# Hybrid decoder step on one core: the factors of four group norms sent as rows through DRAM instead of broadcast products, with new queue orders

## The chip, the core and the metric

The kernel runs on one core of one Trainium2 chip. A core has TensorE (PE, matmul and transpose, with its weight loads shown apart as PEld), VectorE (DVE), ScalarE (ACT), GpSimd (POOL) and SyncE (SP, which here only issues DMAs), each with an instruction queue of its own that runs in order. The metric is the device time in microseconds (us) of one execution. The time of the kernel before is 1998.02 us, the median of 3 runs (1997.06 to 2000.51).

## The reference

One layer of a decoder, for a prompt of 2048 tokens and 8 sample tokens with caches, model width 1024, all in fp32:

```
xn = rmsnorm(x, norm1_g)
xr, gr, q, k, v = split(xn @ w_in)              # 512, 512, 512, 128, 128 columns
rec = rglru(conv4(xr), ...) * gelu(gr)          # per-token scan, block-diagonal gates
att = sliding_window_attention(q, k, v, sinks)  # 8 heads, 2 kv heads, window 128
mix = concat(rmsnorm(rec, rec_norm_g), rmsnorm(att, attn_norm_g))
h   = x + mix @ w_out
hn  = rmsnorm(h, norm2_g)
y   = h + (silu(hn @ w_gate) * (hn @ w_up)) @ w_down
out = rmsnorm(y, final_norm_g)
```

The two norms inside `mix`, called group norms here, are what the change touches: each divides a token's 512 features by the root of their mean square (plus 1e-6) and multiplies by a gain per feature.

## The kernel before, in words

**Layout.** Features lie on the 128 partitions, tokens on the free axis. A tile of 128 features by some 512 tokens is called a chunk; `rec`, `att` and the like have four chunks c = 0 to 3. An fp32 product is done as three fp32r products of high and low parts (high·high, high·low, low·high), so every operand is split into a high part (a copy to fp32r on ScalarE) and a low part (the difference, mostly on VectorE).

**Stages.** The 2056 tokens are four sub-sequences s = 0 to 3: the first holds 512 prompt tokens and the 8 sample tokens (520, run as two blocks of 260), the others 512. Each goes through the input projection (14 units of 128 columns: 0 to 3 the recurrent branch, 4 to 7 the gelu gate, 8 keys, 9 values, 10 to 13 queries), the recurrence, the attention, the two group norms and the output projection (8 units). Work of neighbouring sub-sequences is interleaved, so that TensorE has, for instance, units of s = 1 while the norms of s = 0 are under way. This takes about the first 600 us. Then comes the FFN over three groups of tokens ("halves"), 11 pairs of 128-wide slices each, with sums of operands that save products, and the final norm.

**A group norm** (`group_norm`, line 1515 on). For one s and one group, named `rc` (recurrent) or `at` (attention):

1. ScalarE squares the four chunks, GpSimd adds them up.
2. `rstd_cols`: TensorE multiplies each stretch of w tokens by a column of averages (records named `st_...`), which leaves one factor per token, tokens on partitions, as w × nt numbers (w = 104, nt = 5 for s = 0, else 128 and 4). VectorE adds 1e-6 (line 1125) and GpSimd raises to the power −0.5 (line 1126). The result is `rccols` or `atcols`.
3. The factor of each token must now stand in all 128 partitions, tokens along the free axis. Line 1532 chooses between two ways. `row_bcast` does it on TensorE: nt products of one column, read as a w × 128 matrix, with the identity (records `bc_rc`, `bc_at`), into one PSUM bank of a pool that has only that bank (`ps_m`), and a ScalarE copy to SBUF (line 1140). A bank holds 512 numbers, so s = 0 needs four products, a copy, a fifth product and a second copy; the fifth product waits until the first copy has freed the bank. `dram_bcast` does it by DMA: one TensorE transpose (`tr_rc`, `tr_at`), a ScalarE copy of the nt × w row (line 1149), a DMA of the row to DRAM (line 1150), and a DMA that reads it back into 128 partitions (line 1156). Both DMAs are issued from SyncE.
4. For each chunk: VectorE multiplies by gain and factor (line 1542), ScalarE copies the high part (line 1544), VectorE subtracts for the low part (line 1545). High and low part are the operand `mix` chunk that the output projection reads, recurrent chunks as k = 0 to 3, attention chunks as k = 4 to 7.

Before, only the recurrent norms of s = 1 and s = 2 went through DRAM; the other six group norms used products. The norm of the input (`x`) of s = 1 to 3 and part of the final norm (`f`) use rows as well. For s = 3 the attention factor is applied late, behind the output projection.

```
def rows_out(row, cols, w, nt, name):
    ps = m_tile(f"tr_{name}")
    tr(f"tr_{name}", ps[:nt, :w], cols, ident[:w, :w])
    v = rowp.tile([8, P], F32, tag="row", name=f"row_{name}")[:nt, :w]
    nc.scalar.copy(v, ps[:nt, :w])
    nc.sync.dma_start(row.rearrange("o (j p) -> (o j) p", p=w), v)
...
    nc.sync.dma_start(out[:, :w * nt], row.to_broadcast([P, w * nt]))
```

**The order of the work.** The instruction streams are made by generators with planned times, but the final order on each of the five queues is written out by hand in the table `ORDER` (TensorE from line 107, VectorE 547, ScalarE 668, GpSimd 750, SyncE 787), and `order_engines` ties each instruction to the one before it. A key names a stream: `rn0` and `an0` are the recurrent and the attention norm of s = 0 (DMAs too), `ip1_7_0` an input unit of s = 1, `op0_0_0` an output unit of s = 0, `r13` and `g13` a recurrent and a gate chunk, `a111` an attention step, `o01` an output unit's loads and sums, `x2` the input norm of s = 2. So when a sequence of keys is changed, an engine that stands at one instruction keeps all that follow it waiting.

**Around the change, in s = 0.** The profiled execution has the products of the recurrent factor at 195.34 to 196.4 us on TensorE, its first use on VectorE at 198.38, the eps addition of the attention factor at 211.05, its products from 214.55, the fifth product at 219.93, the first use at 220.71, and the first pass of the output projection at 222.65. Weight loads of the next input units (`w_in<-split_w`, line 1054) and raw loads of `w_out` stand on SyncE's queue in the same stretch.

Of the kernel before, what the change touches and what calls it, by code (L numbers as in the profile page):

```python
# [2383 lines left out]
```

## Time and profile before

| | us |
|---|---|
| median of 3 runs | 1998.02 |
| profiled execution, whole | 1999.11 |
| its span | 1997.0 |
| TensorE busy | 1971.0 |
| VectorE busy | 1560.6 |
| ScalarE busy | 981.3 |
| GpSimd busy | 959.8 |

The profile is of one execution. Its span runs from the first to the last recorded instruction; the whole time has 2.1 us more around it. A row of a group of instructions gives line, engine, operation, output <- inputs by the program's names, partitions × elements, count, then the busy time in us and the mean of one in ns, then the idle time of the engine just before such instructions and what ended it. A row of a timeline gives start and length in us, and in brackets the idle time before it with its releaser. A row of waits gives engine, instruction, what it waited for, the total in us, the number of times, and the longest. Matmuls are pipelined, so the lengths of their records overlap. In rows of DMA issues (SPq) the length is that of the issue and not of the transfer. The mean granted TensorE clock of the run is 0.997 of full speed.

### The profile page before, as it was taken

What the parts mean: (1) busy time and instruction counts of PE and PEld (TensorE: products, weight loads), DVE (VectorE), ACT (ScalarE), POOL (GpSimd) and SP (SyncE); (2) the same over time, 40 slices, a digit from 0 to 9 for tenths busy, and PEclk for the clock granted to TensorE, in tenths of its full rate; (3) what the DMA queues carried; (4) which work ended last, traced back from release to release, by engine and by line L of the source; (5) the groups of instructions that cost most, each with busy time, mean ns of one, the idle gap of its engine ahead of it and who ended that gap; (6) DMA issues with size and microseconds to landing.
All of it is one profiled execution on the core that took longest, in us unless ns stands there. A gap on an engine that the chain in (4) does not pass through costs nothing. (4 is left out here: it accounts for less than half of the span.)

```text
span 1997.0 us, 34846 instructions
## 1 busy us (share of the span) xinstructions
PE 1971.0 (99%) x12112; PEld 1874.8 (94%) x12112; DVE 1560.6 (78%) x2894; ACT 981.3 (49%) x2032; POOL 959.8 (48%) x821
## 2 busy tenths in 40 slices
PE   8999999999999999999999999999999999999998
PEld 8988898888877999999999999999999999999998
DVE  7887986777986888888998786886668586766776
ACT  6775774664664534444446433433345433433433
POOL 5412362130233896788998754534456423322323
PEclk9999999999999999999999999999999999999999
DMA  8873586576688978655667886776558675565552
GB/s 314 287 252 138 194 300 198 183 254 210 223 283 291 335 263 268 220 215 210 246 241 279 265 289 231 234 237 210 191 191 267 228 259 199 179 211 195 180 181 103
DMA packets 218470, 461.93 MB, mean 231 GB/s; under 512 B 26230, under 2 KB 90406, under 8 KB 218278
## 3 DMA queue, kind: packets, MB, share of 16 engines
q1 hardware_dynamic: 214662, 456.69, 67.4%
q10 hardware_dynamic: 3632, 3.02, 0.4%
q8 instruction: 95, 1.56, 0.3%
q14 instruction: 81, 0.66, 0.1%
HBM read 345.51 MB, written 115.17 MB: 231 GB/s over the span
## 5 line engine op out<-in xcount | busy, mean ns | idle before, releaser
L1070 PE MATMUL ps_g<-hn,w_g 128*128 128x342 f32 (+1 forms) x2772 | 569.4, 320 | 0.3 <-DMA w_g<-split_g 0.3
L1070 PE MATMUL ps_u<-hn,w_u 128*128 128x342 f32 (+1 forms) x2772 | 559.5, 320 | 1.5 <-DMA w_u<-split_u 0.9
L1070 PEld LDWEIGHTS ps_g<-hn,w_g 128*128 128x128 f32 x2772 | 461.3, 188 | 1.2 <-ACT wd L1972 0.5
L1070 PEld LDWEIGHTS ps_u<-hn,w_u 128*128 128x128 f32 x2772 | 459.5, 188 | 3.0 <-ACT c_u L2115 1.6
L2175 DVE TENSOR_TENSOR y<-y,pw 128x342 f32<-128x342 f32 (+1 forms) x756 | 359.1, 504 | 114.7 <-PE pw L1070 108.4
L1070 PE MATMUL ip<-xn,w_in 128*128 128x512 f32 (+1 forms) x1680 | 365.2, 357 | 6.1 <-ACT xn L1105 5.7
L1070 PEld LDWEIGHTS ip<-xn,w_in 128*128 128x128 f32 x1680 | 269.6, 189 | 45.8 <-ACT xn L1105 5.7
L1070 PE MATMUL pw<-fh,wd 128*128 128x342 f32 (+1 forms) x864 | 253.4, 320 | 0.5 <-DVE y L2175 0.5
L1070 PE MATMUL pw<-t,wd 128*128 128x342 f32 (+1 forms) x972 | 243.7, 320 | 2.8 <-DVE y L2175 2.7
L1070 PE MATMUL op<-mix,w_out 128*128 128x512 f32 (+1 forms) x960 | 205.8, 355 | 0.4 <-ACT mix L1544 0.4
L1070 PEld LDWEIGHTS op<-mix,w_out 128*128 128x128 f32 x960 | 157.5, 189 | 25.3 <-ACT mix L1544 0.8
L1070 PEld LDWEIGHTS pw<-t,wd 128*128 128x128 f32 x972 | 169.9, 188 | 4.9 <-DVE y L2175 4.0
L1973 POOL TENSOR_TENSOR wd<-rd,wd 128x512 fp32r<-128x512 f32 x85 | 121.8, 1434 | 103.4 <-ACT wd L1972 99.1
L1972 ACT CAST wd<-rd 128x512 fp32r<-128x512 f32 x159 | 98.6, 621 | 130.0 <-PE ps_u L1070 39.8
L1070 PEld LDWEIGHTS pw<-fh,wd 128*128 128x128 f32 x864 | 158.6, 188 | 1.2 <-DVE y L2175 0.8
L1904 POOL TENSOR_TENSOR w_u<-ru,w_u 128x512 fp32r<-128x512 f32 x44 | 61.4, 1395 | 170.2 <-ACT w_u L1903 95.9
L1070 PE MATMUL pw<-fl,wd 128*128 128x342 f32 (+1 forms) x432 | 132.9, 320 | 0.0
L2089 DVE TENSOR_TENSOR c_u<-c_u,ps_u 128x342 f32<-128x342 f32 (+1 forms) x99 | 50.2, 508 | 101.2 <-PE ps_u L1070 93.9
L2071 POOL TENSOR_TENSOR c_u<-c_u,c_g 128x342 f32<-128x342 f32 (+1 forms) x60 | 65.4, 1090 | 124.8 <-DVE c_u L2089 115.1
L2060 DVE TENSOR_TENSOR fl<-c_u,fh 128x342 fp32r<-128x342 f32 (+1 forms) x132 | 105.4, 803 | 17.7 <-ACT fh L2059 17.0
L2059 ACT CAST fh<-c_u 128x342 fp32r<-128x342 f32 (+1 forms) x132 | 63.0, 480 | 110.6 <-POOL c_u L2071 49.3
L1070 PE MATMUL pd<-fh,w_d 128*128 128x344 f32 (+1 forms) x384 | 92.9, 320 | 0.0
(319 smaller groups left out, 3490.7 us busy)
## 6 DMA issues: line engine op xcount, KB each, us to landing
w_g<-split_g SPq DMA_DIRECT2D x88, 512.0 KB
w_u<-split_u SPq DMA_DIRECT2D x88, 512.0 KB
w_in<-split_w SPq DMA_DIRECT2D x84, 512.0 KB
rg<-in_wgate SPq DMA_DIRECT2D x110, 256.0 KB
ru<-in_wup SPq DMA_DIRECT2D x110, 256.0 KB
w_out<-split_w SPq DMA_DIRECT2D x48, 512.0 KB
split_g<-w_g SPq DMA_DIRECT2D x44, 512.0 KB
split_u<-w_u SPq DMA_DIRECT2D x44, 512.0 KB
```

The lines of the kernel that those rows point to most:

```text
L1070: r = nc.tensor.matmul(*args, **kw)
L1904: lo_eng.tensor_tensor(w[:, 1, :], src, w[:, 0, :].bitcast(F32), op=ALU.subtract)
L1972: nc.scalar.copy(w[:, :, 0], v)
L1973: eng((E_DLO0, E_DLO1, E_DLO2)[gi][j]).tensor_tensor(w[:, :, 1], v, w[:, :, 0].bitcast(F32), op=ALU.subtract)
L2059: nc.scalar.copy(hi, v)
L2060: nc.vector.tensor_tensor(lo, v, hi.bitcast(F32), ALU.subtract)
L2071: (nc.vector if p == NPAIR - 1 or src is not v else eng(E_MUL[2 * h + n])).tensor_tensor(v, src, g, op=ALU.mult)
L2089: nc.vector.tensor_tensor(o, a, b, op)
L2175: nc.vector.tensor_tensor(v, v, ps, ALU.add)
```

## The change

Line 1532 chooses the way through DRAM for all group norms but the recurrent one of s = 3 and the late one (the attention norm of s = 3). So the attention norms of s = 0, 1 and 2 and the recurrent norm of s = 0 change from products to rows; the recurrent norms of s = 1 and 2 went through DRAM already.

```diff
-                bc = (dram_bcast if name == "rc" and s in (1, 2) else row_bcast)(cols[:w, :nt], w, nt, f"{name}{s}")
+                bc = (row_bcast if late or name == "rc" and s == 3 else dram_bcast)(cols[:w, :nt], w, nt, f"{name}{s}")
```

The table `ORDER` is written anew for all five engines. TensorE's list loses the 18 products `bc_at0`, `bc_at1`, `bc_at2`, `bc_rc0` and gains the four transposes; ScalarE's loses two entries (the second copies of s = 0); SyncE's gains eight (a write and a read for each of the four norms). All else is the same set of instructions in another order: of some 11,960 entries of TensorE 1357 stand elsewhere relative to the others, of VectorE's 2766 it is 745, of ScalarE's 1885 it is 402, of GpSimd's 817 it is 109, of SyncE's 1495 it is 304. The moves lie at the start (x loads, splits and the first input units), around the border of s = 0 and s = 1, and at some places in the FFN.

Around s = 0's norms, VectorE's list (`rn0` the four products and four low parts of the recurrent norm, `an0` first the eps addition and then products and low parts):

```diff
-a100+1 a100:3 a031 r11 a101+2 a101+2 v1 k2+1 a101:2 a111 k2+1 a101:2 a100 v1 a101:3 a110 a100 v1 a110:3 a120 rn0 a101
-a110:4 r12 a110 a111:4 rn0+6 rn0 a121 rn0+1 rn0 rn0+1 a111 a101 a111+1 rn0 g10 rn0+1 r10 g10 g11 r11 a111+1 rn0 g10
-r10 r11 g11 an0 r11 g11 r13 a111 g12 a111 g12 an0 an0+1 an0+2 an0 g13 g12 an0 an0+1 g13 an0:2 x2+1 x2 a100 o00:2 r11
+a100 a100+1 a100:3 a031 r11 a101+2 a101+2 v1 k2+1 a101:2 a111 k2+1 a101:2 a100 v1 a101:3 a110 a100 v1 a110:3 a120 rn0
+a101 a110 a110+1 a110+1 a110:2 a111:2 r12 a101 a111 a121 a111:2 a111+2 a111+2 a111+1 a111 r10 rn0 rn0+1 rn0 rn0+1 g10
+rn0 rn0+1 rn0 g10 g11 rn0 g10 r10 r11 g11 an0 r11:2 g12 g11 r13 g12 g13 g12 an0 an0+5 an0+1 an0 an0+1 an0:3 x2:2 a100
```

TensorE's list at the same places:

```diff
-s5_1_0:3 ip1_2_0 s5_1_1 ip1_2_0 pt4_1_1 s5_1_1 pt4_1_1:2 ip1_2_0 bc_rc0_0 s5_1_1 bc_rc0_0:3 pt4_1_1 ip1_5_0:2 o4_0_1
-ip1_5_0 bc_rc0_4 o4_0_1 s6_0_0 ip1_5_0:2 g1_0_0_0:2 ip1_6_0 g1_0_0_0 ip1_6_0:2 ip1_5_0 ip1_6_0:7 g1_0_1_0 ip1_6_0
...
-ip1_6_0 st_at0 ip1_3_0:4 st_at0 ip1_3_0:20 ip1_7_0:2 s6_0_1 ip1_7_0:3 pt5_0_0 ip1_7_0 bc_at0_0:4 ip1_7_0:7 pt5_0_0
-ip1_7_0 bc_at0_4 ip1_7_0:8 op0_0_0:2 ip1_7_0:2 g1_1_0_0 op0_0_0 g1_1_0_0 op0_0_0 g1_1_0_0 op0_0_0:8 op0_0_260:9
...
+s5_1_0 s5_1_1 s5_1_0:2 s5_1_1 ip1_2_0:2 pt4_1_1 s5_1_1 pt4_1_1:2 s5_1_0 s5_1_1 pt4_1_1 tr_rc0 ip1_2_0 ip1_5_0:2 o4_0_1
...
+ip1_6_0 st_at0 pt5_0_0 st_at0 pt5_0_0 s6_0_1 pt5_0_0 ip1_3_0:24 ip1_7_0:12 tr_at0 ip1_7_0:10 op0_0_0:2 ip1_7_0:2
```

SyncE's list there: the recurrent norm's write and read (`rn0:2`) stand ahead of the weight loads `r13:2 g13:2`, the attention norm's (`an0:2`) behind them.

```diff
-r12:2 g12:2 o01+3 r13:2 g13:2 o01+1 o00 o02 o00 o02+1 o01 o03 o01 o02 o03+1 x2:2 o04 o00 o04+1 o03 x2 o02+1 o01 o02 x2
+r12:2 g12:2 o01+3 rn0:2 r13:2 g13:2 an0:2 o01+1 o00 o02 o00 o02+1 o01 o03 o01 o03+1 o02 x2:2 o04 o00 o04+1 o03 o02 o01
```

More of the change, by code (lines that the diff above doesn't have):

```diff
@@ new lines @@
+vt0_0 ip0_3_0:6 ip0_3_1 ip0_3_0:2 ip0_3_1:4 ip0_11_0 vt0_1 ip0_3_1:13 ip0_11_0:6 ip0_3_1 vt0_2 ip0_3_1:4 ip0_11_0:7
+ip0_11_1 vt0_3 ip0_11_1:7 g0_0_0_0:2 ip0_11_1:4 g0_0_0_0 ip0_11_1:2 ip0_10_0:2 ip0_11_0 ip0_11_1:2 ip0_11_0
+g0_0_0_260:3 ip0_11_0:5 ip0_11_1 ip0_11_0 g0_0_1_0:3 ip0_11_0:2 ip0_10_0:4 ip0_11_1:4 g0_0_1_260:3 ip0_11_1:3
+ip0_10_0:3 ip0_10_1 ip0_10_0:5 ip0_10_1:7 ip0_10_0:9 ip0_10_1 ip0_10_0 ip0_10_1:13 ip0_13_0:2 ip0_10_1:2 ip0_13_0:12
+ip0_13_1:4 ip0_13_0:3 ip0_13_1:4 ip0_13_0:7 ip0_13_1:11 ip0_2_0 ip0_13_1:3 ip0_2_0 ip0_13_1:2 ip0_2_1:3 ip0_2_0:3
@@ new lines @@
+pt14_1_1:2 op2_7_0 pt14_1_1 op2_7_0:2 s15_1_1 op2_7_0:5 o14_1_0 op2_7_0:3 o14_1_0 op2_7_0:2 o14_1_1 st_rc3:4 op2_7_0
+o14_1_1 pt15_0_0:4 op2_7_0:4 bc_rc3_0:4 op2_7_0:2 pt15_0_1:4 op2_7_0 o15_0_0:2 o15_0_1 pt15_1_0:4 o15_0_1 st_h2:4
+pt15_1_1:4 o15_1_0:2 op3_0_0 op3_1_0 op3_2_0 op3_0_0:2 op3_1_0 o15_1_1 op3_2_0 op3_1_0:2 tr_h2 o15_1_1 op3_0_0
+op3_2_0:2 op3_1_0 op3_0_0 op3_1_0 op3_0_0:2 op3_2_0:2 op3_0_0:2 op3_1_0:2 op3_2_0:2 op3_1_0 op3_2_0:2 op3_0_0:3
+op3_1_0 op3_2_0 op3_1_0:2 op3_2_0 op3_3_0:12 op3_4_0:12 st_at3:2 op3_5_0:12 st_at3:2 op3_6_0:9 op3_7_0 op3_6_0:2
@@ new lines @@
+d0_1_6_0 d0_1_6_1 u0_2_1 d0_1_6_0:3 d0_1_7_0 d0_1_6_0 d0_1_7_0 d0_1_7_1 d0_1_7_0 d0_1_6_0 d0_1_7_0 d0_1_7_1:2
+d0_1_7_0:2 d0_1_7_1 u0_2_1 d0_1_7_1 u0_2_1 u0_2_2 u0_2_1 u0_2_2 d0_1_7_1 u0_2_2:3 u0_2_1 u0_2_2:7 u0_2_5:7 u0_2_6:2
+u0_2_5:3 u0_2_6 u0_2_5 u0_2_6:8 g0_3_1 u0_2_6 g0_3_1:3 u0_2_5 g0_3_1:7 u0_2_7 g0_3_1 u0_2_7:7 u0_2_3 u0_2_7 u0_2_3
+u0_2_7:3 u0_2_3:8 g0_3_6:2 u0_2_3 g0_3_6 u0_2_3 g0_3_6:9 u0_2_4:12 g0_3_2:10 d0_2_0_0 g0_3_2 d0_2_1_0 d0_2_0_0
+d0_2_0_1 d0_2_0_0 g0_3_2 d0_2_1_0:2 d0_2_0_1:2 g0_3_5 d0_2_1_1 g0_3_5 d0_2_1_1:2 g0_3_5:8 d0_2_0_1 d0_2_0_0 g0_3_5
@@ new lines @@
+w1_1_2_1 w1_1_1_2 w1_1_2_1 w1_1_1_3 g1_2_4 w1_1_1_2:2 g1_2_4:2 w1_1_1_3 g1_2_4 w1_1_4_1 g1_2_4 w1_1_4_1 w1_1_4_0
+g1_2_4 w1_1_4_1 w1_1_4_0 g1_2_4:3 w1_1_4_0 u1_2_1:2 g1_2_4 u1_2_1 g1_2_4:2 u1_2_1:3 w1_1_6_3 w1_1_6_2:2 u1_2_1:2
+u1_2_2:2 w1_1_6_3 w1_1_5_2 w1_1_6_2 w1_1_6_3 w1_1_5_2 w1_1_5_3 w1_1_5_2 w1_1_5_3:2 u1_2_1:2 u1_2_2 u1_2_1 u1_2_2
+u1_2_1 u1_2_2:6 w1_1_7_2 u1_2_2 w1_1_7_2 w1_1_7_3 w1_1_7_2 w1_1_3_2:2 w1_1_7_3 w1_1_3_2 w1_1_3_3 w1_1_7_3 w1_1_3_3
+w1_1_2_2:3 u1_2_6 u1_2_2 u1_2_6:2 w1_1_3_3 u1_2_6:7 w1_1_4_2 u1_2_6 w1_1_4_3 w1_1_4_2 u1_2_6 u1_2_5:2 w1_1_4_3
@@ new lines @@
+w2_9_2_2 u2_10_4:2 w2_9_4_2 w2_9_4_3 w2_9_4_2:2 w2_9_4_3:2 d2_10_0_1:2 u2_10_4 d2_10_1_1 d2_10_0_1:3 d2_10_1_1:5
+d2_10_2_1 d2_10_0_1 d2_10_2_1 d2_10_3_1 d2_10_2_1:2 d2_10_4_1 d2_10_2_1:2 d2_10_3_1:4 d2_10_4_1 d2_10_3_1 d2_10_5_1
+d2_10_4_1:4 d2_10_5_1 d2_10_6_1 d2_10_5_1:4 d2_10_6_1:5 d2_10_7_1:6 d2_10_0_0:5 d2_10_1_0:4 st_f2_1:6 d2_10_0_0
+d2_10_1_0:2 d2_10_2_0:3 bc_f2_1:3 d2_10_2_0:3 d2_10_3_0:6 d2_10_4_0:4 d2_10_5_0 d2_10_4_0:2 d2_10_5_0:3 d2_10_6_0
+d2_10_5_0:2 d2_10_6_0:5 d2_10_7_0:6 w_st_f2_0:9 w_bc_f2_0:3 st_f2_0:6 bc_f2_0:3
@@ L745 @@
[L745 to L748 removed]
+pre x0:2 pro+1 x0+1 x0+1 x0+2 x0+5 x0:2 x0+1 x0+2 x0+3 x0+5 x0+4 v0 x0+5 r01+1 x0 xs1 pre x0:4 v0 x0 k0 pro xs1 k0
```

1356 lines of the change are left out of this document (665 added, 691 removed).

## The prediction

> **What bounds the kernel now.** I read first the page, then the waits of TensorE, then a table by windows, and last the timelines around the places that the change touches.
>
> ```profile
> PE 1971.0 (99%) x12112; PEld 1874.8 (94%) x12112; DVE 1560.6 (78%) x2894; ACT 981.3 (49%) x2032; POOL 959.8 (48%) x821
> ```
> ```profile
> PE ip L1070 <- ACT xn L1105: 5.7, 1, 5.7
> PE pw L1070 <- DVE y L2175: 3.3, 5, 1.2
> PE bc_at L1070 <- ACT rb_at L1140: 2.4, 1, 2.4
> ```
> TensorE is busy nearly all of the 1997.0 us span. Its longest stall is the start; the longest inside the run is one stand of 2.4 us, before a product named bc_at, which the change takes out. So the time falls by what TensorE no longer issues, by that stand, and by what follows it; and it rises by whatever TensorE will then wait for.
>
> ```profile
> 217.60:219.90 2.30, 0.00 (x0) 0.00 (x0) 1.80 (x5) 1.02 (x2) 0.00 (x0) 1.00 0.79 312
> 221.50:224.80 3.30, 3.30 (x11) 2.72 (x10) 2.55 (x5) 2.71 (x5) 1.55 (x3) 0.50 0.00 0
> 200.00:300.00 100.00, 97.65 (x652) 88.70 (x651) 87.73 (x158) 74.80 (x147) 47.75 (x43) 0.98 0.72 248
> ```
> After the length come the busy times of TensorE, its weight loads, VectorE, ScalarE and GpSimd, then the granted clock, the share of the DMA engines and GB/s. TensorE stands for 2.3 us, and soon after it runs 3.3 us at half clock. In the stage 200 to 300 us VectorE is busy 87.7%: it has little room of its own, which matters below.
>
> **What is taken out of TensorE.** 18 products go: five each for the attention and the recurrent norm of sub-sequence 0, four each for the attention norms of 1 and 2. Four transposes come. Each fp32 product is two records.
>
> ```profile
> L1070 PE MATMUL bc_at<-cs,atcols 128*128 128x128 f32 (+1 forms) x34 | 5.3, 276 | 2.4 <-ACT rb_at L1140 2.4
> L1070 PE MATMUL bc_rc<-cs,rccols 104*128 104x104 f32 (+1 forms) x18 | 2.6, 271 | 0.0
> ```
> ```profile
> 439.77 1.80 PE L1070 MATMUL op<-mix,w_out 128*128 128x512 f32 x7
> 441.40 0.27 PE L1075 MATMUL tr_rc<-cs,rccols 128*4 128x128 f32 x1
> ...
> 594.18 0.94 PE L1070 MATMUL op<-mix,w_out 128*128 128x512 f32 x3
> 594.96 1.05 PE L1070 MATMUL bc_rc<-cs,rccols 128*128 128x128 f32 x8
> 595.77 0.94 PE L1070 MATMUL op<-mix,w_out 128*128 128x512 f32 x3
> ```
> Removed are 26 of the 34 bc_at records and 10 of the 18 bc_rc records. By busy time that is 26/34 of 5.3 and 10/18 of 2.6: 5.5 us. But records overlap, so I go by starts. Seven op passes take 441.40 − 439.77 = 1.63 us, 0.233 each. From 594.18 to 595.77 are 1.59 us, three op passes (0.70) and eight records of bc_rc: 0.111 each. 36 × 0.111 = 4.0 us. Four transposes at the same 0.11 are 0.45 us (at most 4 × 0.27 = 1.1 by the row at 441.40). All of it lies on TensorE, which has no other idle time to absorb it.
>
> **What goes with the stand.**
>
> ```profile
> 211.05 0.15 DVE L1125 TENSOR_SCALAR atcols<-st_at 104x5 f32<-104x5 f32 x1
> 211.83 5.47 DVE L1520 SCALAR_TENSOR_TENSOR rrec<-gt,rrec 128x512 f32<-128x512 f32 x1
> ...
> 220.71 2.10 DVE L1542 SCALAR_TENSOR_TENSOR ratt<-ratt,vec,rb_at 128x520 f32<-128x520 f32 x3 [0.50 <-ACT rb_at L1140]
> 228.30 2.41 DVE L1545 TENSOR_TENSOR mix<-ratt,mix 128x520 fp32r<-128x520 f32 x2
> ```
> ```profile
> 211.28 1.61 POOL L1126 TENSOR_TENSOR atcols<-atcols,nhalf 104x5 f32<-104x5 f32 x1 [14.42 <-DVE atcols L1125]
> 212.86 2.51 POOL L1044 TENSOR_TENSOR w_out<-raw_out,w_out 128x512 fp32r<-128x512 f32 x2
> ```
> ```profile
> 218.85 0.63 ACT L1517 ACTIVATE gt<-rrec 128x512 f32<-128x512 f32 x1 [6.34 <-DVE rrec L1434]
> 219.39 0.49 ACT L1140 COPY rb_at<-bc_at 128x416 f32<-128x416 f32 x1
> ```
> ```profile
> 219.93 0.47 PE L1070 MATMUL bc_at<-cs,atcols 104*128 104x104 f32 x2 [2.35 <-ACT rb_at L1140]
> ...
> 222.65 0.64 PE L1070 MATMUL op<-mix,w_out 128*128 128x260 f32 x2
> ```
> The fifth product needs the one bank of that pool, which the copy of the first four frees at 219.4 to 219.9. The copy stands on ScalarE behind a gelu step, and that one behind a VectorE operation that took 5.47 us while GpSimd ran without a break. With the rows there is one bank turn and no second copy, so the stand of 2.4 us goes. If no stand of this length takes its place, the 3.3 us at half clock go too: half of them is lost time, 1.7 us.
>
> The Trainium skill has a rule on that: "TensorE: Matmul & The Clock Gate", the section on the clock gate, says that the rate halves only after at least one whole idle window of about 3.4 us. By that rule a stand of 2.3 us should have cost no clock, and the sum below would be 1.7 us smaller. The trace differs from it, and I go by the trace.
>
> Without new waits the sum is 4.0 − 0.45 + 2.4 + 1.7 = 7.6 us: 6.1 in sub-sequence 0 (20 records 2.2, two transposes −0.2, stand 2.4, clock 1.7) and 1.6 in sub-sequences 1 and 2.
>
> **What the rows add.** Per norm: a transpose, a small ScalarE copy, and two DMAs on SyncE's queue, the read waiting until the write has landed. Two such trips of before had a consumer waiting for their end:
>
> ```profile
> 122.89 0.29 SPq L1150 DMA_DIRECT2D rows_x<-row_x  x1
> ...
> 125.82 0.32 SPq L1156 DMA_DIRECT2D rb_x<-rows_x  x1
> ...
> 1578.42 0.26 SPq L1150 DMA_DIRECT2D rows_f<-row_f  x1
> ...
> 1579.87 0.32 SPq L1156 DMA_DIRECT2D rb_f<-rows_f  x1
> ```
> ```profile
> 131.88 0.69 DVE L1434 TENSOR_TENSOR kraw<-ip,rb_x 128x512 f32<-128x512 f32 x1 [0.33 <-DMA rb_x<-rows_x]
> 1583.15 1.06 DVE L2195 SCALAR_TENSOR_TENSOR y<-y,vec,rb_f 128x342 f32<-128x342 f32 x2 [0.77 <-DMA rb_f<-rows_f]
> ```
> From the issue of the write to the consumer: 131.88 − 122.89 = 9.0 us and 1583.15 − 1578.42 = 4.7 us. The windows above show the DMA engines at 0.79 up to 219.9 us and at 0.00 from 221.5 to 224.8, so a broadcast at 220 finds them soon free: I take 6 us, nearer to the lower row, and keep both ends.
>
> The Trainium skill's page "DMA: Bandwidth & Descriptors", in its anatomy of a transfer, gives each about 2.0 us plus bytes over 436 GB/s and so speaks against splitting work into small transfers. An estimate from it, for a row and a 266 KB broadcast, is 2.0 + 2.6 = 4.6 us, the lower end of the two rows; by it first products would stand about 1.4 us earlier than I assume.
>
> Sub-sequence 0's recurrent norm: the transpose can stand where the products stood, at 195.34 in before; with the small copy the row write is issued at about 196.0, and its rows are in at 200.7 to 205.0.
>
> ```profile
> 195.34 0.37 PE L1070 MATMUL bc_rc<-cs,rccols 104*128 104x104 f32 x2
> ```
> ```profile
> 198.38 1.43 DVE L1542 SCALAR_TENSOR_TENSOR rrec<-rrec,vec,rb_rc 128x520 f32<-128x520 f32 x2
> ```
> ```profile
> 190.20 13.13 SPq L1054 DMA_DIRECT2D w_in<-split_w  x4
> ```
> The new VectorE order puts 7 to 14 other operations ahead of these four products; seven of about 0.68 us (the row at 131.88 is one of their kind) place the first at about 203.1 instead of 198.38. These products' results are read from 222.65 on, so the delay costs TensorE nothing itself. What it pushes is queued behind it on VectorE: the eps addition of the attention norm, which I place at 212.7 instead of 211.05, an estimate: of the operations moved ahead some wait for TensorE, which comes no sooner, so VectorE stands for some 1.7 us that it doesn't stand now. On SyncE the two DMAs stand ahead of the weight loads of the row at 190.20, which slip to about 198.6; the first user of those weights is at about 206, so a margin of 2 to 3 us covers it.
>
> Sub-sequence 0's attention norm: 212.7 + 0.15, then GpSimd's 1.6 (row at 211.28), transpose and copy: the write is issued at about 215.8. Rows in at 220.5 (4.7) to 224.8 (9.0), 221.8 at my 6 us. So the first attention product comes at about the time it had, 220.71, or 1 us later, while TensorE comes 6.1 us earlier. The last low part of before ended at 228.30 + 2.41 = 230.71, 10.0 us behind the first product. After, fewer gate operations stand between, and I allow 7.5 to 8.5 us: 229.3 to 230.3.
>
> ```profile
> 231.16 3.24 PE L1070 MATMUL op<-mix,w_out 128*128 128x260 f32 x25
> ```
> By the written order that last low part is read about the fifteenth pass of this block, at 232.9. So before had a slack of 2.2 us there, and 6.1 us are taken from it: TensorE arrives at 226.8 and waits until 229.3 to 230.3, which is 2.5 to 3.5 us in all, spread over the four chunks in pieces below 2.4, so without the clock. With 0.3 for other small waits behind the crowded VectorE, about 3.3 us of the 7.6 come back. Forecast: a gain of 4.3 us.
>
> Sub-sequences 1 and 2 gain 0.8 us each; VectorE delivers their attention halves several us before they are read, so the trip hides there. The rest of the change is order alone: at the start it moves x loads and splits, in the FFN it shifts neighbours by a few places. I cost both at nothing; the five waits of the row "DVE y L2175", 3.3 us in all, can go or come again, so ±2 us stay for the range.
>
> **The rivals.** (A) Full gain: the trips take about 4.7 us and VectorE, no longer starved as in the 5.47 us row, catches up; nothing stands. −7.6: 1990.4. For it: the starvation goes if GpSimd's run falls elsewhere. Against: the slack of 2.2 us.
>
> (B) The gain is used up in sub-sequence 0: the second trip takes 7 to 9 us, rows at 222.8 to 224.8, the last low part at about 232. TensorE waits some 5.5 us, in one piece long enough for half clock again, 1.7 more. −7.6 + 7.2 = −0.4: 1997.6. For it: the trip of 9.0 us. Against: that of 4.7.
>
> (C) Slower: VectorE stands in order at the first recurrent product. It decides from a first trip over 203.1 − 196.0 = 7.1 us. At 9.0 us VectorE stands 1.9 us, everything queued behind it slips, the attention row is written at 217.7, and after another 9.0 us the first product is at 226.7, the last low part 10 us later at 236.7 against 226.8: 9.9 us of waits and 1.7 of clock, and up to 1.9 of late gate steps. 13.5 − 7.6 = +5.9 at most, +4 without the gate steps; I take 2002.5.
>
> (D) The half clock at 221.5 does not come from the stand but falls where it falls, and stays: everything else as forecast, 1.7 less gain, 1995.4. For it: it begins 1.6 us after the stand has ended. Against: it occurs nowhere else in the run outside its two ends. The Trainium skill's clock page, in the same section, calls the window free-running, and under its rule the stand of 2.3 us cannot have been the whole cause.
>
> (E) The order alone moves the start or the FFN by more than the two norms do: either sign, 1990 to 2003, by the 3.3 us of small waits and the 5.7 us of the start's.
>
> **How the numbers follow.** Chances: forecast 0.42, A 0.19, B 0.22, C 0.08, D 0.05, E 0.04. The profiled execution took 1999.11 us, its span 1997.0 and 2.1 around it; the sum gives it 1994.8. The median of the runs is 1998.02, so its forecast is 1998.02 − 4.3 = 1993.7. About 0.2%, 4.0 us, is what a measurement of this kernel can tell from no change: faster means below 1994.0, slower above 2002.0. The forecast's own range, from the trip's two ends and the ±2 us, is 1991 to 1996.5; a little over half of it counts as faster, all of A, none of B, C or D, a quarter of E. Faster 0.42 × 0.57 + 0.19 + 0.01 = 0.44, slower C and a quarter of E, 0.09, the same 0.47. The range reaches to A's full gain and B: 1990.0 to 1998.0, which leaves C and parts of A and E out.
>
> **What would show it.** Right: no record of bc_at before the late sub-sequence; no wait on L1140 near 220; TensorE waiting in pieces of 0.3 to 2 us for mix or ratt of L1542 to L1545 between 222 and 232, near full clock there; rb_at of sub-sequence 0 landing 5 to 7 us after its row was issued. Wrong: no such waits (A); one piece above 2.3 us followed by half clock (B); VectorE idle before L1542 near 203 for rb_rc (C); half clock near 221 without a stand (D); a difference that arises before 190 us or after 600 us (E).

## The result and the profile after

Over 18 runs each, on the same chips, the changed kernel takes 2004.34 us (median; 1998.51 to 2007.77) and the kernel before 2000.50 (1997.06 to 2005.51). The ratio of the times is 1.0015 (as of the means, 2003.78 and 2000.70; the medians lie further apart), 95% interval 1.0008 to 1.0022: 3.0 us slower (1.6 to 4.4), where 4.3 us faster was forecast, and within the 0.2% that the prediction calls the same. The profiled execution of the changed kernel took 2000.47 us, its span 1998.7.

Its page and its waits of TensorE, to be read beside those of before (line numbers are lower by two in the changed kernel, and by up to fifteen in the experiments, whose tables are wrapped otherwise):

```profile
PE 1971.8 (99%) x12080; PEld 1873.8 (94%) x12080; DVE 1562.1 (78%) x2894; ACT 982.6 (49%) x2030; POOL 968.8 (48%) x821
```
```profile
PE ip L1068 <- ACT xn L1103: 5.6, 1, 5.6
PE pw L1068 <- DVE y L2173: 4.0, 5, 1.1
PE pt L1073 <- DVE ptl L1659: 1.6, 4, 0.7
PE op L1068 <- DVE mix L1543: 1.0, 1, 1.0
PE bc_rc L1068 <- POOL rccols L1124: 0.8, 1, 0.8
PE op L1068 <- POOL w_out L1042: 0.6, 1, 0.6
```
32 records fewer, and the same busy time; the wait of bc_at is gone, and smaller ones stand in its place. What the first line hides is in the windows view, whose third column from the right is the granted clock (cut here at three stretches):

```profile
225.40:228.40 3.00, 3.00 (x14) 2.81 (x14) 2.92 (x3) 2.98 (x6) 2.96 (x2) 0.50 0.42 152
600.50:603.50 3.00, 3.00 (x10) 2.38 (x9) 2.90 (x6) 2.17 (x5) 1.22 (x1) 0.50 0.32 101
1601.50:1604.50 3.00, 3.00 (x13) 3.00 (x13) 3.00 (x8) 0.00 (x0) 0.00 (x0) 0.58 0.76 219
```
Three stretches at half clock inside the run, of 3.4 us each and so 1.7 us lost each; before had one.

Around the norms of sub-sequence 0 the timeline after (TensorE, SyncE's issues, VectorE):

```profile
213.88 0.26 PE L1073 MATMUL tr_at<-cs,atcols 104*5 104x104 f32 x1
217.04 0.48 PE L1068 MATMUL op<-mix,w_out 128*128 128x260 f32 x2 [0.56 <-ACT xch L1467]
222.45 0.39 PE L1068 MATMUL op<-mix,w_out 128*128 128x260 f32 x1 [0.61 <-POOL w_out L1042]
224.29 1.70 PE L1068 MATMUL op<-mix,w_out 128*128 128x260 f32 x9 [0.98 <-DVE mix L1543]
```
```profile
194.65 0.27 SPq L1148 DMA_DIRECT2D rows_rc<-row_rc  x1
214.44 0.27 SPq L1148 DMA_DIRECT2D rows_at<-row_at  x1
```
```profile
201.89 1.43 DVE L1540 SCALAR_TENSOR_TENSOR rrec<-rrec,vec,rb_rc 128x520 f32<-128x520 f32 x2
211.39 0.16 DVE L1123 TENSOR_SCALAR atcols<-st_at 104x5 f32<-104x5 f32 x1
220.51 3.12 DVE L1540 SCALAR_TENSOR_TENSOR ratt<-ratt,vec,rb_at 128x520 f32<-128x520 f32 x3
224.83 4.09 DVE L1543 TENSOR_TENSOR mix<-ratt,mix 128x520 fp32r<-128x520 f32 x3
```
The first pass of the output projection moved from 222.65 to 217.04; the attention products on VectorE stayed where they were (220.71 before, 220.51 now); TensorE then waits for them.

**Lead by stage.** The tables below are worked out by me, in us: the start of each TensorE pass in a kernel's trace less the start of the same pass in before's, as the median over the passes within 6 us of a mark, and its change from mark to mark. Negative is time gained against before's profile. An "h" stands for each half-clock stretch of 3.4 us within the stage ("hh": two, one right behind the other). Before's own profile has one at 221, so a kernel that does the same work there without it shows −1.55.

| kernel | 60–150 | 150–230 | 230–330 | 330–531 | 531–610 | 610–700 | 1100–1200 | 1580–1640 |
|---|---|---|---|---|---|---|---|---|
| changed | −1.31 | −1.98 h | +1.63 | −1.44 | +2.59 h | +1.24 | −1.43 | +1.29 h |

The start gains 1.3 us by order alone, sub-sequences 1 and 2 gain 1.4, sub-sequence 0 nothing to speak of (−1.98 + 1.63 = −0.35), and behind 531 us more is lost than was gained.

### The profile page after: what moved, and what is told of

It is laid out like the page before. It is cut to its first block, busy times and chain, and to the rows that moved or that the text cites. A ratio compares the mean times of both kernels' runs of the same rounds, so it can differ in the third digit from the quotient of the medians.

```text
span 1998.7 us, 34792 instructions
## 1 busy us (share of the span) xinstructions
PE 1971.8 (99%) x12080; PEld 1873.8 (94%) x12080; DVE 1562.1 (78%) x2894; ACT 982.6 (49%) x2030; POOL 968.8 (48%) x821
## 4 chain that ended last, share of the span: by engine, by line
PE 92%; DVE 4%; DMA 3%; ACT 0%; issue 0%; SPq 0%; POOL 0%; DVEq 0%; ACTq 0%; POOLq 0%
PE ps_g L1068 22%; PE ps_u L1068 21%; PE pw L1068 18%; PE ip L1068 14%; PE op L1068 7%; PE pd L1068 5%; PE s L1068 1%; PE o L1068 1%; PE pt L1073 1%; PE g L1068 1%; DVE xc L1455 1%; DMA out_yT<-y 1%; DMA m<-mixed 1%; DMA hs<-xres 0%; DVE q L1498 0%
```

## The experiments

All kernels below carry the orders of before or of after in whole stretches, cut where both lists have issued the same instructions on an engine, and say at the line that sets `bc` (1532 in the changed kernel) which norms go by rows. In the diffs below, lines that begin with ORDER, a kernel or an engine tell the edit in words; the others are code.

### Which stretch gains and which loses

e1: new orders and rows only from 150 to 330 us, around the norms of sub-sequence 0.

```diff
-bc = (dram_bcast if name == "rc" and s in (1, 2) else row_bcast)(cols[:w, :nt], w, nt, f"{name}{s}")
+bc = (dram_bcast if (name, s) in [('at', 0), ('rc', 0), ('rc', 1), ('rc', 2)] and not late else row_bcast)(cols[:w, :nt], w, nt, f"{name}{s}")
-ORDER of before
+ORDER of before to 150 us, of after from 150 to 330, of before behind
```


> The kernel before, with the new orders and the two rows (recurrent and attention norm) only in the stretch from 150 to 330 us, around the norms of sub-sequence 0. Theory 1 (the gain of sub-sequence 0 is given back on the spot: TensorE comes 6 us earlier, waits some 2 us for the attention half of mix, loses 1.7 us to half clock and 1.6 us more at 263 to 275): TensorE is 0 to 1 us ahead of before at 330 us, and the time is within 1 us of before. Theory 2 (sub-sequence 0 does gain, and the loss comes from the new orders elsewhere): 4 to 6 us ahead at 330 us, ratio 0.997 to 0.998.

e2: the reverse.

```diff
-ORDER of after
+ORDER of after to 150 us, of before from 150 to 330, of after behind; rows: ('at', 1), ('at', 2), ('rc', 1), ('rc', 2)
```


> The changed kernel, with the old orders and the products for the two norms of sub-sequence 0 in the stretch from 150 to 330 us; the attention norms of 1 and 2 by rows, the new orders before and after. Theory 1: ahead of before by 1.2 us at 150 us, by 1.2 at 330, by 2.7 at 530, and 0 to 1 us slower than before at the end, as the changed kernel is. Theory 2: slower than the changed kernel by some 4 us, ratio to before 1.003 or more.

e3: all four norms by rows, new orders up to 531 us.

```diff
-ORDER of after
+ORDER of after to 531 us, of before behind
```


> All four norms by rows and the new orders up to 531 us, the old orders behind that. Theory A (the new orders behind 531 us cost the 3.6 us that are lost there): 3 us ahead at 531 us and still 2.5 to 3 us ahead at 720 us and at the end, ratio 0.9985. Theory B (whoever comes 3 us earlier waits there, for VectorE and GpSimd are the limit between 580 and 630 us): the lead falls to between 0 and 1 us by 720 us also with the old orders, ratio 1.000.

e4: the changed kernel, unaltered.

> The changed kernel once more, unaltered, for a second profile. If the half-clock windows follow from the waits alone, they fall at the same three places (225, 600 and 1600 us, 1.7 us each). If it depends on how the waits fall against a window that runs on its own, places and number change while the waits stay, and the time with them by 1.7 us for each window.

| kernel | ratio to before (95%) | 60–150 | 150–230 | 230–330 | 330–531 | 531–610 | 610–700 | 1100–1200 | 1580–1640 |
|---|---|---|---|---|---|---|---|---|---|
| e1 | 1.0012 (1.0001–1.0022) | +0.08 | −2.69 | +2.52 | 0.00 | +0.84 h | +0.47 | −0.37 | +0.37 |
| e2 | 1.0018 (1.0009–1.0028) | −1.36 | +0.04 h | +0.16 | −1.48 | +4.31 hh | +0.62 | −0.33 | +1.29 h |
| e3 | 0.9996 (0.9987–1.0006) | −1.37 | −2.77 | +2.46 | −1.47 | +4.79 hh | −0.29 | −0.05 | +0.50 |
| e4 | 1.0024 (1.0014–1.0033) | −1.37 | −2.95 | +2.53 | −1.47 | +3.62 h | +0.61 | +1.11 h | +1.92 |

Theory 1 holds for sub-sequence 0: in e1, e3 and e4 TensorE is ahead by 2.7 to 3.0 us at 230 and by 0.2 to 0.4 at 330, with no half clock there. The changed kernel's first profile had half clock at 225 and ends at the same place (−0.35): where TensorE stands at 330 does not depend on it. The time fits less well: e1 was to be within 1 us of before and is 2.4 us slower (0.2 to 4.4). Theory 2, a gain in sub-sequence 0, fell: by it e2, which does without the rows there, was to be 4 us slower than the changed kernel, and is at 1.0018 against e4's 1.0024.

e3 and e4 differ only in the orders behind 531 us, and are 0.9996 and 1.0024 of before: 0.0028, or 5.6 us, lie there. Theory A is right about these orders, but not as it was put: its 0.9985 lies outside e3's interval, and e3 kept no lead past 610 in its profile either, 3.4 us of it lost to half clock. There TensorE stood for a load:

```profile
602.15 0.48 ACT L1239 CAST hn<-m 128x344 fp32r<-128x344 f32 x1 [2.08 <-DMA m<-mixed]
```
```profile
603.20 2.93 PE L1056 MATMUL op<-mix,w_out 128*128 128x512 f32 x6 [1.59 <-ACT mix L1530]
```
ScalarE stands in order at a cast whose load has not landed; the high part of mix that TensorE needs is queued behind. e2 and e4 show the same wait (1.5 and 1.4 us), before 0.35. But kernels below come as early and don't wait there, so theory B isn't general either.

e4 answers its own question: half clock fell at 602 and 1155, not at 225 and 1600. Its waits at 223 to 225 were 0.60 and 0.98, as in the first profile.

### The new orders behind 531 us, alone

f1: new orders from 720 us only, products and old orders before that; f2: new orders from 531 to 720 only.

```diff
-ORDER of before
+f1: ORDER of before to 720 us, of after behind
+f2: ORDER of before to 531 us, of after from 531 to 720, of before behind
```


> The kernel before up to 720 us, products and all, and the new orders from 720 us on (nearly all of the FFN). Theory E (the new orders in the FFN cost time of their own): level with before up to 1100 us, then 1 to 3 us of waits and half clock between 1130 and 1160 or 1595 and 1620 us, ratio 1.001 to 1.002. Rival (the FFN's losses in the changed kernel's profiles are chance): within 0.5 us of before at 1980 us apart from half-clock windows that before shows as often, ratio 1.000.

> The kernel before up to 531 us and from 720 us on, the new orders between. If the 2.6 to 3.6 us that the changed kernel loses at 585 to 610 us come from the new orders there, they are lost here too: ratio 1.0015. If they come from the lead of TensorE meeting a fixed landing time of the load of mixed near 602 us, nothing is lost here but a half-clock window at times: 0 to 1.7 us at 720, ratio 1.000 to 1.0005.

h1 is f1 with the old orders put back at the two places where the FFN passes from one token group to the next; h2 and h3 divide f2's stretch.

```diff
-ORDER of f1
+h1: ORDER of before from 1105 to 1185 and from 1570 to 1635 us, the rest as f1
-ORDER of f2
+h2: ORDER of after from 531 to 610 us alone
+h3: ORDER of after from 610 to 720 us alone
```


> f1 (new orders from 720 us on) with the old orders put back on all engines from 1105 to 1185 and from 1570 to 1635 us. Theory (the FFN's loss lies at these two handovers, where VectorE's new order has one or two more products ahead of the sums that TensorE waits for): TensorE waits there as in before, 0.16 to 0.17 us instead of 0.65 for the second sum at 1600, and is within 0.5 us of its place at 720 at the end but for a half-clock window; ratio 1.000. Rival (the loss is spread over the FFN): 1 us or more lost elsewhere, ratio 1.001.

> The kernel before with the new orders from 531 to 610 us alone. If the wait for the power on GpSimd ahead of the last recurrent factor's products (0.7 us in f2, none in before) is what costs: 0.3 to 0.8 us lost by 610 us and kept, ratio 1.0003.

> The kernel before with the new orders from 610 to 720 us alone. f2 lost 1.8 us there, with a wait of 0.33 us near 679 that all kernels with these orders have and none with the old ones: 1 to 2 us lost between 610 and 700 us, ratio 1.0005 to 1.001. If it was chance: nothing lost, ratio 1.000.

| kernel | ratio to before (95%) | 150–230 | 531–610 | 610–700 | 700–1100 | 1100–1200 | 1580–1640 |
|---|---|---|---|---|---|---|---|
| f1 | 1.0012 (1.0003–1.0021) | −1.55 | +0.14 | −0.02 | +0.39 | +1.58 | +1.72 h |
| f2 | 1.0014 (1.0003–1.0024) | +0.01 h | +0.59 | +1.75 | −0.17 | −0.38 | −0.33 |
| h1 | 1.0004 (0.9995–1.0013) | −1.57 | +1.33 h | +0.18 | +1.11 | +0.58 | −0.36 |
| h2 | 1.0011 (1.0000–1.0023) | −1.53 | +0.04 | −0.27 | +0.03 | +0.24 | +0.74 |
| h3 | 1.0003 (0.9994–1.0012) | −1.55 | +0.02 | +1.39 | +0.05 | +0.27 | −0.51 |

f1 came out as theory E has it. f2's ratio is the one that was named for a loss at 585 to 610 us, but its profile loses 1.75 us from 610 to 700 and only 0.59 by 610. The times add up: 2.4 us of f1 and 2.8 of f2 are 5.2 of the 5.6 between e3 and e4. Not every column can be read from one profile: between 1100 and 1200 us kernels with the new orders show −1.43, −0.33, +1.11 with a half clock and +1.58, and those with the old ones −1.09 to +0.58.

The orders cost time where nothing of the norms is near. At 1600 us the reason can be read. VectorE, then TensorE, in f1:

```profile
1596.90 2.52 DVE L2180 SCALAR_TENSOR_TENSOR y<-y,vec,rb_f 128x342 f32<-128x342 f32 x5 [2.61 <-DMA rb_f<-rows_f]
1599.33 0.51 DVE L2160 TENSOR_TENSOR y<-y,pw 128x342 f32<-128x342 f32 x1
1599.75 1.06 DVE L2180 SCALAR_TENSOR_TENSOR y<-y,vec,rb_f 128x342 f32<-128x342 f32 x2
1600.72 0.51 DVE L2160 TENSOR_TENSOR y<-y,pw 128x342 f32<-128x342 f32 x1
```
```profile
1599.89 0.74 PE L1055 MATMUL pw<-t,wd 128*128 128x342 f32 x3 [1.73 <-DVE y L2160]
1601.29 1.22 PE L1055 MATMUL pw<-t,wd 128*128 128x342 f32 x3 [0.65 <-DVE y L2160]
```
and in h1, which has the old orders there:

```profile
1601.65 0.50 DVE L2161 TENSOR_TENSOR y<-y,pw 128x342 f32<-128x342 f32 x1
1602.07 0.56 DVE L2181 SCALAR_TENSOR_TENSOR y<-y,vec,rb_f 128x342 f32<-128x342 f32 x1
1602.56 0.50 DVE L2161 TENSOR_TENSOR y<-y,pw 128x342 f32<-128x342 f32 x1
```
```profile
1602.20 0.74 PE L1056 MATMUL pw<-t,wd 128*128 128x342 f32 x3 [1.25 <-DVE y L2161]
1603.11 0.74 PE L1056 MATMUL pw<-t,wd 128*128 128x342 f32 x3 [0.16 <-DVE y L2161]
```
The sum y<-y,pw frees the result bank that TensorE's next three passes need. The new VectorE order puts two products ahead of the second sum, the old one a single one: 0.65 us of waiting against 0.16. The changed kernel, e2, e4 and f1 all wait 0.65 at the second sum, no kernel with the old orders does. Such a wait just behind a first of 1 to 1.7 us also comes with half clock more often: in 3 of these 4 profiles against 2 of 13 with the old orders there. In the stage 1580–1640 the four lose 1.3 to 1.9 us. In three of them half clock alone is 1.7, all of their loss or more; the fourth, e4, loses 1.9 without it. So of the longer wait itself no loss is seen in those three stages: what the new orders cost there is above all clock.

The runs that were not profiled bear that out. The mean granted clock of the four kernels with the new orders all through the FFN (the changed kernel, e2, e4, f1) is 0.9947 to 0.9959, that of the twelve others 0.9963 to 0.9977. f1 is at 0.9959 against 0.9970 in the runs of before beside it: 2.2 of its 2.4 us. h1, with only the two handovers put back, is at 0.9973 against 0.9967.

h1's theory holds at 1600, and its stage shows −0.36; its whole ratio of 1.0004 cannot be told from none, nor quite from f1's, and 1.1 us were lost between 700 and 1100 us in its profile, which none of this explains.

Between 610 and 700 us all profiles with the new orders lose 0.6 to 1.75 us (the changed kernel, e2, e4, f2, h3), those with the old ones between −0.35 and +0.5. h3 alone shows it, with the wait that all five have:

```profile
677.74 4.56 PE L1055 MATMUL ps_g<-hn,w_g 128*128 128x344 f32 x26 [0.33 <-DVE c_u L2074]
```
This wait and one of 0.20 us at 626.78 are nearly all the idle time that h3 has there; where the rest of its 1.39 us goes is open. Its time, 0.6 us slower (1.2 faster to 2.4 slower), cannot tell the 1 to 2 us that were expected from nothing. h2's theory of the wait for GpSimd's power is refuted as a cost: the wait is there (0.51 us) and nothing is lost by 610. Its ratio of 1.0011 is not visible in its profile, nor in its mean clock (0.9966, before 0.9967), and stays unexplained; so how f2's 2.8 us divide at 610 is open too.

### Why sub-sequence 0 does not gain

f3 and f4 leave out the same six VectorE operations, two taps of the convolution in each of three chunks of sub-sequence 1 (so `xc` lacks these two terms); f3 is otherwise the kernel before and f4 is e1.

```diff
-                for j in (1, 2, 3):
+                for j in ((3,) if s == 1 and c else (1, 2, 3)):
```


> The kernel before without six VectorE operations: two of the three later taps of the convolution in the chunks 1 to 3 of sub-sequence 1 are left out, some 5 us of VectorE work between 205 and 270 us. It is the control of the next run: 0 to 2 us ahead of before at 330 us, the wait of the fifth product near 217 as before or shorter.

> The first experiment's kernel (new orders and rows only around the norms of sub-sequence 0) without the same six VectorE operations. Theory 1 (VectorE, 95% busy from 220 to 270 us, decides where TensorE stands at 300): with 5 us less of it, 3 to 5 us more of TensorE's lead of 5 us at 224 survive, so it is 3 us or more ahead of the control at 330. Rival (TensorE is held by a load or by GpSimd): the lead still goes, and it is within 1 us of the control at 330.

g1 moves one copy on ScalarE in the kernel before; g2 is the kernel before with rows for the attention norm of sub-sequence 0 alone.

```diff
-ACT: ... r11 g12 an0:2 g12 an0 ...
+ACT: ... r11 an0 g12 an0 g12 an0 ...
```


> The kernel before with one move: on ScalarE the first copy of the attention factor of sub-sequence 0 stands one place earlier, ahead of the gelu square that waited for the starved VectorE operation. If that copy alone made the stand of 2.35 us, the stand goes, no half clock follows it, and TensorE is 2.3 us ahead at 330 us of a before without half clock (4.0 of one with it), with neither rows nor new orders: ratio 0.998 to 0.999. If VectorE is the limit there whatever TensorE does, the lead goes by 300 us: ratio 1.000.

```diff
-PE: bc_at0_0 (four times) ... bc_at0_4
+PE: tr_at0 at the place of the first
-ACT: ... r11 g12 an0:2 g12 an0 ...
+ACT: ... r11 an0 g12 g12 an0 ...
-SP: g13:2 o01+1
+SP: g13:2 an0:2 o01+1
```


> The kernel before with rows for the attention norm of sub-sequence 0 alone: transpose where the products stood, old orders on all engines, the two DMAs at the place on SyncE that the change gives them. If the rows land by 221 us, where VectorE takes its first product in the old order, TensorE saves 1.1 us of products and the stand of 2.35 and waits 1 to 2 us for the last low parts: 1.5 to 2.5 us ahead at 330 of a before without half clock, ratio 0.9985. If the trip is what spoils it, VectorE stands at the first product for 1 us or more, TensorE waits over 3 us for mix, nothing is gained: ratio 1.000 or above.

| kernel | ratio to before (95%) | 150–230 | 230–330 | 531–610 | 610–700 |
|---|---|---|---|---|---|
| e1 (again) | 1.0012 (1.0001–1.0022) | −2.69 | +2.52 | +0.84 h | +0.47 |
| f3 | 0.9994 (0.9983–1.0005) | −2.67 | +0.26 | +2.51 hh | −0.12 |
| f4 | 0.9995 (0.9983–1.0007) | −2.20 h | +0.35 | +1.87 h | −0.33 |
| g1 | 0.9997 (0.9988–1.0006) | −3.53 | +1.18 | −0.35 | −0.29 |
| g2 | 0.9998 (0.9989–1.0007) | −2.02 h | +0.58 | +1.29 h | −0.33 |

f4 against f3 missed what theory 1 expected: −1.85 and −2.41 at 330, no 3 us between them, partly since f4 had half clock (1.7) and partly since the control gained by the same means, its stand at 219 shrinking to 1.17. The numbers are those that the rival named. But the lead that the rival says must go did not go: e1 loses 2.52 us between 230 and 330, f4 0.35; the changed kernel's first profile, with half clock at the same place as f4's, loses 1.63. So it is VectorE's work there that takes most of e1's lead. How, its rows in e1 show:

```profile
263.52 0.84 DVE L1476 SCALAR_TENSOR_TENSOR q<-q,ra 128x512 f32<-128x512 f32 x1
264.29 1.82 DVE L1442 SCALAR_TENSOR_TENSOR xc<-xr,vec,xc 128x512 f32<-128x512 f32 x1
266.04 0.68 DVE L1646 TENSOR_TENSOR ptl<-pt,pth 128x512 fp32r<-128x512 f32 x1
```
```profile
266.86 0.41 PE L1060 MATMUL pt<-cs,sc 128*128 128x128 f32 x2 [0.77 <-DVE ptl L1646]
```
The low part of the transposed attention weights (ptl) stands behind two recurrent operations, one of them at 1.82 us instead of 0.75, and TensorE waits for the bank that it frees. In f4, where that operation (xc) is left out, ptl comes right behind the first of the two, and TensorE doesn't wait for it:

```profile
261.71 0.83 DVE L1476 SCALAR_TENSOR_TENSOR q<-q,ra 128x512 f32<-128x512 f32 x1
262.46 0.68 DVE L1646 TENSOR_TENSOR ptl<-pt,pth 128x512 fp32r<-128x512 f32 x1
```
Four waits for VectorE behind 230 us, which f4 hasn't, are idle time of 1.36 us in e1: 0.21 and 0.21 at 232 to 234, 0.77 and 0.17 at 267 to 274. The rest of the 2.52 us is no idle time in the records. In f1, with the old orders, ptl comes at 263.10 and TensorE doesn't wait. That is again order, for with the old orders a lead of 1.55 us lasts from 230 to 531 (f1, h1, h2, h3).

g1 takes away the stand of 2.35 us and nothing else, and shows what it was worth. TensorE's rows:

```profile
217.96 0.36 PE L1056 MATMUL bc_at<-cs,atcols 104*128 104x104 f32 x2
224.77 0.50 PE L1056 MATMUL g<-xch,gwh 128*128 128x512 f32 x1 [0.30 <-ACT ra L1464]
229.74 2.54 PE L1056 MATMUL op<-mix,w_out 128*128 128x260 f32 x19 [0.67 <-DVE mix L1531]
```
The late copy was the cause of the stand, as the prediction has it. The passes right behind the stand come 2.62 us earlier, 0.27 more than the idle time in its row; in f3, where the stand is shorter by 1.18 and not gone, they come 1.18 earlier. So a wait can cost TensorE more than its row shows. But at 330 TensorE is only 2.35 us ahead of before's profile, that is 0.8 ahead of an execution of before without half clock (f1, h1 to h3 stand at −1.4 to −1.55 there), where 2.3 were expected. The rest went in the two waits of the last rows, 0.30 for ScalarE and 0.67 for VectorE, which the stand had covered. In the times nothing of it can be told from chance.

g2's rows, write and read on SyncE and the first product on VectorE:

```profile
216.16 0.27 SPq L1136 DMA_DIRECT2D rows_at<-row_at  x1
217.33 0.33 SPq L1142 DMA_DIRECT2D rb_at<-rows_at  x1
```
```profile
221.66 2.10 DVE L1528 SCALAR_TENSOR_TENSOR ratt<-ratt,vec,rb_at 128x520 f32<-128x520 f32 x3 [0.43 <-DMA rb_at<-rows_at]
```
The trip takes 5.5 us and VectorE stands 0.43 for it, less than the 1 us that was to spoil it; TensorE then waits 1.81 us for ScalarE and gets half clock behind it, and at 330 it is level with a before without half clock, where 1.5 to 2.5 us ahead were expected. The row's copy stands ahead of the gelu square here, as g1's copy does. Rows alone in the old orders are neither gain nor loss; the 0.9985 of the first theory lies outside the interval.

### The parts that gained, put together

g3: new orders to 150 us, old ones and products for sub-sequence 0, rows and new orders for the attention norms of 1 and 2, old orders from 531. g4: the same with g1's copy.

```diff
-ORDER of after
+ORDER of after to 150 us, of before to 330, of after to 531, of before behind; rows: ('at', 1), ('at', 2), ('rc', 1), ('rc', 2)
+g4: and ACT: ... r11 an0 g12 an0 g12 an0 ...
```


> The parts of the change that gained in the profiles: the new orders up to 150 us (1.4 us), rows for the attention norms of 1 and 2 with the new orders from 330 to 531 us (0.75 each); old orders and products for the norms of sub-sequence 0 and old orders behind 531 us. 2.9 us ahead at 531; if the landing of mixed near 602 us takes the lead back, level at 720 and ratio 1.000; if not, 0.9985.

> The kernel of g3 with the moved copy of g1 as well: 5.2 us ahead at 531 us of a before without half clock. With what is kept behind 602 us: ratio 0.9975 if the leads last, 0.999 to 1.000 if the landing of mixed takes them back.

| kernel | ratio to before (95%) | 60–150 | 150–230 | 230–330 | 330–531 | 531–610 | 610–700 |
|---|---|---|---|---|---|---|---|
| g3 | 0.9997 (0.9988–1.0006) | −1.37 | 0.00 h | +0.13 | −1.49 | +0.31 | −0.30 |
| g4 | 0.9992 (0.9983–1.0000) | −1.35 | −3.53 | +1.46 | −1.49 | +1.83 h | −0.29 |

The two gains of 1.4 and 1.5 us are there in every kernel that has them. Both leads last through 602 us but for a half clock, so the landing of mixed is not a fixed barrier; it held e2, e3 and e4 and not these. g4 is better than the changed kernel (0.9992 against 1.0015 and 1.0024), and against before its interval ends at no change; the 0.9975 that was expected lies outside it. At 531 us g4 was to be 5.2 us ahead of a before without half clock and is 3.4, for the moved copy nets 0.5 us here and 0.8 in g1. In g3's times 0.6 us of the 2.9 are seen, and its interval, 2.4 us faster to 1.2 slower, does not reach 2.9; where the rest goes in the executions that were not profiled is open.

## Why the prediction was wrong, point by point

**Right.** Rows in place of products in sub-sequences 1 and 2: 1.6 us forecast, 1.44 to 1.49 in six kernels. The late first ScalarE copy as the cause of the stand (g1). The places on VectorE: taking off the 1.25 us that the changed profile is ahead at 150, the first recurrent product was to come at 203.1 and came at 203.1, the eps addition at 212.7 and came at 212.6; the attention row was to be written at 215.8 and, so corrected, went at 215.7. The trip: 6 us forecast, 5.5 in g2 and 6.3 in e1 (217.02 to 223.33), where VectorE stood for it, at most 6.1 in the changed kernel (214.44 to 220.51, with no wait for it). The Trainium skill's page "DMA: Bandwidth & Descriptors" gives the figure behind the estimate of 4.6 us for a DMA issued from GpSimd (its anatomy of one DMA); these are issued from SyncE, and 5.5 to 6.3 differs from it.

**The half clock, 1.7 us of the gain.** The step "if no stand of this length takes its place, the 3.3 us at half clock go too" counted one execution's chance as a cost of the stand. Eight kernels here have that stand of 2.30 to 2.35 us: four profiles show half clock behind it (before, e2, f2, g3) and four don't (f1, h1, h2, h3). So the term was worth about half of 1.7. f1's rows:

```profile
219.54 0.47 PE L1055 MATMUL bc_at<-cs,atcols 104*128 104x104 f32 x2 [2.30 <-ACT rb_at L1125]
```
```profile
219.50:223.00 3.50, 3.46 (x18) 2.94 (x19) 3.00 (x6) 2.66 (x6) 0.13 (x1) 1.00 0.07 27
```
And shorter waits can bring it too: 0.61 and 0.98 us within 2.5 us did so in the changed profile, 0.65 and 0.98 in f4, and waits like these (0.60 to 0.86, and 0.97 or 0.98) did not in e1, e3 or e4. So its return had to be expected at every cluster of waits.

What decides can be worked out from the traces' record of the granted clock. In every profile the half-clock stretches inside the run begin a whole number of 3.413 us behind the first rise to full clock (in the changed kernel 63, 173 and 466 of them): there is a fixed grid, which lies elsewhere in each execution. Of the stand, 1.89, 2.30, 2.10 and 2.30 us fall into one window of this grid in before, e2, f2 and g3, and at most 1.41, 1.39, 1.74 and 1.54 in f1, h1, h2 and h3. The window with the most of it in before, and the two that share it in f1 (the second number is TensorE's busy time, the clock is the third from the right):

```profile
218.04:221.45 3.41, 1.52 (x8) 1.31 (x9) 2.41 (x6) 1.80 (x4) 0.00 (x0) 1.00 0.55 220
```
```profile
215.24:218.65 3.41, 2.00 (x10) 1.33 (x8) 3.39 (x5) 0.19 (x1) 1.12 (x1) 1.00 0.83 295
218.65:222.06 3.41, 2.52 (x13) 2.17 (x14) 2.43 (x4) 2.56 (x6) 0.00 (x0) 1.00 0.32 131
```
Over all 17 profiles each of the seven windows with over 1.75 us idle is followed by half clock, six of the ten with 1.5 to 1.75, and below that none but those near 600 us, where 0.8 to 1.4 us were enough (and less for the second of two stretches in a row); why so little there, no run shows. Rival D, that the half clock falls where it falls, was right about the grid and not about the stand: it falls behind waits. The Trainium skill's page "TensorE: Matmul & The Clock Gate", in its section on the clock gate, has a free-running window of 3413 ns, and half rate after at least one idle window. The window agrees with these traces; that it must be wholly idle does not.

**The size of what comes back in sub-sequence 0.** Forecast were 3.3 us of 7.6, "with 0.3 for other small waits behind the crowded VectorE". The 2.5 to 3.5 us of it that were to be waits for mix came to 0.98 in the changed profile and 1.2 in e1, e3 and e4; the waits that the prediction doesn't name were larger in sum, for ScalarE (0.56), for a split of w_out on GpSimd (0.60 to 0.86), and for VectorE behind 230 us, where the new order puts ptl behind starved operations. In sum e1, e3 and e4 wait 3.45 to 3.76 us, near the 3.3 by luck. But the sum took a wait for no more than its idle time. Without any half clock 4.4 us were taken out here in the prediction's terms (products 2.2 less transposes 0.2, stand 2.4), and against executions of before without half clock sub-sequence 0 is 1.1 to 1.4 us slower in the kernels with the new orders: 5.5 to 5.8 us came back. About 2 us of that stand in no row as idle time. Seven waits at the 0.27 us by which g1's stand was dearer than its row would be 1.9, an estimate from that one stand. Against the half of the executions of before that have half clock, sub-sequence 0 is 0.2 to 0.4 us faster. And the stand's 2.4 us was no free gain either: g1 nets 0.8 of it.

**The order elsewhere, costed at nothing.** This failed most. The start gained 1.35 us. The stretch 610 to 700 lost 0.6 to 1.75, and at 1600 us 0.5 us was added to a wait and half clock made likelier, far from any norm. e3 and e4 put a price on the orders behind 531 us: 5.6 us. Of these, 3.0 are clock: the mean granted clock over 10 executions is 0.9971 in e3 and 0.9956 in e4, and 0.0015 of 2000 us is 3.0. Of the other 2.6, by the profiles, about 1 lies between 610 and 700 and up to 0.5 in the longer wait at 1600; the last 1 us I can't place. This is rival E, to which I gave 0.04: it had its own sign in three places, and the sum of them is what the result is.

**The forecast's range** (1990 to 1998) fell with these: 1.35 gained at the start, 1.45 in sub-sequences 1 and 2, about 0.5 lost in sub-sequence 0 (the mean of the two comparisons), and behind 531 us 3.0 lost by clock and 2.6 otherwise, is 3.3 us slower; measured 3.0 (1.6 to 4.4). That the two agree so closely is partly luck, for the difference of e3 and e4 is known to some 1.3 us only (the means of their ten runs are 1999.5 and 2004.8).

## What to carry to other kernels

When a change rewrites the order of every queue, cost the order as work of its own: go through each place where an instruction that frees another engine's buffer moves behind something else. One more product ahead of such a sum on VectorE made TensorE wait 0.5 us longer here, far from the edit. A stand on the busiest engine is worth only what is left when the next late input is counted; moving the one copy that caused it tells that at once. And a cost seen once beside a wait, such as a half clock, is a cost with a chance: look for the same wait in other executions before it enters a sum. Count waits as well as adding them up, for one cost more than its row shows.

## What the runs showed of the hardware

Half clock came in stretches of 3.41 us, 1.7 us lost each, zero to four of them inside a run, and at different places in two profiles of the same kernel (225, 600, 1600 and 602, 1155). They began on a grid of 3.413 us that lay elsewhere in each execution, behind windows of that grid with 1.5 us or more of idle time (0.8 or more near 600 us, the second of two stretches in a row aside); a window with over 1.75 us was followed by one each time. The mean granted clock of single executions of the changed kernel ranged from 0.994 to 0.998, worth 8 us, and its times from 1998.5 to 2007.8; but the two go together only loosely, for the slowest execution had 0.996.

Taking away a wait of 2.35 us put TensorE 2.62 us ahead (g1); making it 1.18 us shorter put it 1.18 ahead (f3).

The start of the run varied as well, by up to 1.8 us at 60 us in kernels with the same instructions up to there (f1 0.4 ahead of before's profile, h2 1.3 behind it).

VectorE operations on two SBUF inputs took 0.68 to 0.75 us with GpSimd idle, 1.82 beside one GpSimd operation of 1.29 us (264.29 of e1) and 5.47 while GpSimd ran without a break (211.83 of before). That GpSimd is the cause is read from these rows; no run moved its work.
